# Forgetting attention: VectorE and ScalarE in the order of the program, slabs by halves of 512 tokens, and another split of the PSUM banks

## The chip, the cores and the metric

The kernel runs on one core of a Trainium2 chip. The metric is the device time of one execution in microseconds (us). The profile tells, for each engine of the core, when each instruction ran: PE is TensorE's matmuls and PEld its weight loads, DVE is VectorE, ACT is ScalarE, POOL is GpSimd, and SP issues most of the transfers. Lines such as L180 are lines of the kernel before the change.

## The reference

A trunk of two layers over 1024 tokens of width 1024. Each layer projects its input once into a main branch, memory queries and two gates, runs the main branch and a four-head attention into 256 memory tokens, multiplies both with the SiLU of their gates, projects back and ends in a LayerNorm of `alpha * x + y`. In layer 0 the main branch is a causal pooling over windows of 2, 4, 8 and 16 tokens. In layer 1 it is forgetting attention with 16 heads of 64 channels. Cut to what matters here:

```python
def shared_kv(x, w_kv_shared, b_forget):
    h = x @ w_kv_shared
    k, v = ...                      # 16 heads of 64
    cum = cumsum(log_sigmoid(f_logit + b_forget))
    return k, v, cum

def forgetting_attention(u, k, v, cum):
    logits = einsum('bqhd,bkhd->bhqk', q, k) * 64 ** -0.5
    logits = logits + (cum[t] - cum[s])          # causal: s <= t only
    p = softmax(logits)
    return einsum('bhqk,bkhd->bqhd', p, v)

def mixer_sublayer(x, mem, w_in, w_mem_kv, w_out, main_fn):
    h = x @ w_in                    # [main | mem q | main gate | mem gate]
    y_main, y_mem = main_fn(u_main), memory_attention(q_mem, mem, w_mem_kv)
    y = concatenate([y_main * silu(g_main), y_mem * silu(g_mem)])
    return y @ w_out
```

## The kernel before

**Precision and slabs.** Matmul operands are held as a high and a low part (`hi_lo`: ScalarE casts, VectorE subtracts), and a product is three matmuls: high by high, high by low, low by high. Projections are done in slabs (`slab`): 128 output channels by 1024 tokens, 48 matmuls of 512 columns. A slab's weights come in two pieces of 512 input channels, each a transfer into a `raw` buffer (four of them) and a pair of `w` buffers (six, so three pieces at a time). Outside the attention the pieces are split by ScalarE and VectorE, within it by GpSimd (`gp_hi_lo`, L144 to L146). A slab takes two PSUM accumulators at its start, one for each half of the tokens, and goes through the first piece for both halves, then through the second piece for both.

**PSUM.** There are eight banks: three for slabs (tag `pj`), two for logits (`L`), two for exponentials and transposes (`T`), one for values (`O`).

**Stages.** Layer 0 runs its first pooling group, the memory attention, the other three groups and the output projection with the norm. A pooling group (`pool_group`) is two slabs with a chain of shifted additions on VectorE, two gate slabs, and a mixing of four accumulators of six matmuls each (L518 to L526). Layer 1 runs the memory attention, then a start that makes K and Q of the first pairs of heads, then the attention (`fox`), then `OutProj.rest`. The memory attention and everything from the start of layer 1's heads on has TensorE in the order of the program (`manual_schedule`). VectorE, ScalarE, GpSimd and SP are put in order by the planner of the language, from its own estimates.

**The attention.** `fox` goes through 16 heads, and for each through eight query tiles of 128, from tile 7 down to tile 0. One tile is one step. Heads come in pairs that share slabs of K, Q and V. A step issues `probs`: the mask on the diagonal block of R, the row of forget terms (GpSimd, L716); the logits in one part (up to 512 keys) or two (L722, L723); a VectorE instruction that adds R and takes the running minimum (L724), which reads the logits out of their bank; and after the last part the exponentials on ScalarE into `T` banks, with row sums (L732). `inverse` makes 1/sum of the tile before (VectorE, L740 to L745), and `behind` splits that tile's exponentials into a high half (ScalarE, L753) and a low half (VectorE, L754). `turn` transposes the halves by DMA, and five steps later (`LAG`) `values` multiplies them with V. The values are evicted by ScalarE (L783) and VectorE (L784). Between these, `fill.pump` gives TensorE slab matmuls of the next pair (`pair_units`: a K, a Q and a V slab) and of gates: about 9 to 12 a step. Their evictions are K and Q (`k_evac`, L655 and L656; `q_evac`, L666 and L667), V (a copy, then `scaled_halves`: a maximum, five one-column operations, a high and a low half) and gates (`gate`, L193 and L194). In the last pair the weights of the output projection are split too, with ScalarE and VectorE kept in program order for these alone (`pinned`).

Of the kernel before, what the change touches and what calls it, by code (L numbers as in the profile page):

```python
# [13 lines left out]
I32 = mybir.dt.int32  # L14
# [57 lines left out]
def trunk_kernel(ctx, tc, x, xT, memT, win, wk, wv0, wv, wmk, wmv, wout, poolw, pscale, lng, lnb, bforget, out):  # L72
# [65 lines left out]
    def hi_lo(hi, lo, src, pinned=False):  # L138

        pin = tc.keep_in_program_order if pinned else lambda ins: ins  # L140
        pin(nc.scalar.copy(hi, src))  # L141
        pin(nc.vector.tensor_tensor(lo, src, hi.bitcast(F32), ALU.subtract))  # L142
# [27 lines left out]
    def slab(pieces_dram, XH, XL, evac, banks=("pj", 3)):  # L170

        accs = [ps([P, NH], *banks) for _ in range(2)]
        for pc in range(2):
            ready = isinstance(pieces_dram, list)
            h, l = pieces_dram[pc] if ready else split_w(pieces_dram[pc], [P, 4, P])
            for n in range(2):
                for k in range(4):
                    kt = pc * 4 + k
                    for i, (a, b) in enumerate(((h, XH), (h, XL), (l, XH))):
                        nc.tensor.matmul(  # L180
                            accs[n], a[:, k, :], b[:, kt, n * NH : (n + 1) * NH],
                            start=kt == 0 and i == 0, stop=kt == KT - 1 and i == 2,
                        )
                        if kt == KT - 1 and i == 2:
                            evac(slice(n * NH, (n + 1) * NH), accs[n])
                        since[0] += NH
                        yield NH
# [3 lines left out]
    def gate(acc, dst):  # L191

        nc.scalar.activation(dst, acc, AF.Tanh, scale=0.5)  # L193
        nc.vector.scalar_tensor_tensor(dst, dst, 1.0, acc, ALU.add, ALU.mult)  # L194

    def mem_kv(l):
# [9 lines left out]
        def project(w_dram):  # L206

            acc = ps([P, NH], "pj", 3)[:, :NMEM]
# [16 lines left out]
        def vals(h):  # L225
            scaled_halves(
                project(wmv[l, h]), [two[:, h, 2 * e : 2 * e + 2, :].rearrange("p m t -> p (m t)") for e in range(2)],
                undo[:, h : h + 1],
            )
            if h == MH - 1:  # L230
                nc.sync.dma_start_transpose(v.rearrange("p h b d -> p (h b) d"), two.rearrange("p h b t -> p (h b t)"))
# [3 lines left out]
    def scaled_halves(u, halves, un, by_tile=lambda t: t):  # L235

        m, e, sc = (tiny(1) for _ in range(3))
        nc.vector.tensor_reduce(m, u, AX.X, ALU.max, apply_absolute_value=True)  # L240
        nc.vector.tensor_scalar(m, m, 2.0 ** -100, None, ALU.max)
        nc.vector.tensor_scalar(e.bitcast(I32), m.bitcast(I32), 0x7F800000, None, ALU.bitwise_and)
        nc.vector.reciprocal(sc, e)
        nc.vector.tensor_scalar(sc, sc, 2.0 ** 14, None, ALU.mult)
        nc.vector.tensor_scalar(un, e, 2.0 ** -15 / PSCALE, None, ALU.mult)
        (hi, lo), u = halves, by_tile(u)
        nc.scalar.activation(hi, u, AF.Copy, scale=sc)
        nc.vector.scalar_tensor_tensor(lo, u, sc, hi, ALU.mult, ALU.subtract)
# [14 lines left out]
    def mem_attention(l, XH, XL, kv, qtile, ytile, yd):  # L263
# [18 lines left out]
        def probs(i):  # L282
# [3 lines left out]
            for hp in range(2):  # L286
                lg = ps([P, 2, NMEM], "L", 2)
# [49 lines left out]
    class OutProj:  # L337
# [23 lines left out]
        def split(self, upto, pinned=False):  # L361

            while self.n < upto:
# [6 lines left out]
                hi_lo(h[j], lo[j], self.raws.pop(0), pinned)  # L370
# [19 lines left out]
        def early(self, y, yh, yl):  # L390
# [4 lines left out]
            for two in (slice(0, 2), slice(2, 4)):  # L395
                hi_lo(yh[:, two, :], yl[:, two, :], y[:, two, :], True)
                yield
# [3 lines left out]
        def rest(self, resid, XH, XL, dst):  # L401
# [11 lines left out]
            for sp, c in order + [(sp, c) for sp in range(2, ST // 2) for c in (2, 0, 1)]:  # L413
                if c == 2:
                    accs[sp] = self.open((("T", 2), ("T", 2), ("pj", 3), ("O", 1))) if 0 in accs and sp == 1 else self.open()
# [63 lines left out]
    with tc.tile_pool(name="in0", bufs=1) as in0:  # L479
# [4 lines left out]
        def pool_group(g):  # L484
            w = WINDOWS[g]
            pms = []
            for f in (2 * g, 2 * g + 1):
# [3 lines left out]
                    ("L", 2) if f == 1 else ("pj", 3),  # L491
# [23 lines left out]
            for d in range(2):  # L515
                f = 2 * g + d
                for n in range(2):
                    acc = ps([P, NH], "pj", 3)  # L518
# [24 lines left out]
    with tc.tile_pool(name="in1", bufs=1) as in1:  # L543
# [16 lines left out]
        def values_of(u):  # L560
# [4 lines left out]
            scaled_halves(  # L565
# [3 lines left out]
            for b in range(2):  # L569
                nc.sync.dma_start_transpose(v[:, b, :, :], two[64 * b : 64 * b + 64].rearrange("p s e t -> p (s e t)"))  # L570
# [17 lines left out]
        def v_first():  # L588
# [7 lines left out]
            for s in range(ST):  # L596
                acc = ps([P, NH], "pj", 3)
# [50 lines left out]
        def qk_units(p):  # L648
# [4 lines left out]
            def k_evac(cols, acc):  # L653
                for t, w, (own, other) in zip(ks, ws, halves):
                    nc.scalar.copy(t[own, cols], acc[own, :])  # L655
                    nc.vector.tensor_tensor(t[other, cols], acc[own, :], t[own, cols].bitcast(F32), ALU.subtract)  # L656
                    if cols.stop == S:
                        for to, of in ((own, other), (other, own)):
                            nc.sync.dma_start(w[to, :].bitcast(F32), t[of, :].bitcast(F32))
# [4 lines left out]
            def q_evac(cols, acc):  # L664
                for t, (own, other) in zip(qs, halves):
                    nc.scalar.activation(t[own, cols], acc[own, :], AF.Copy, scale=-0.125)  # L666
                    nc.vector.scalar_tensor_tensor(  # L667
                        t[other, cols], acc[own, :], -0.125, t[own, cols].bitcast(F32), ALU.mult, ALU.subtract,
                    )
# [34 lines left out]
        def probs(hd, i, R, sums, inverse, behind):  # L704
# [16 lines left out]
            for n, (lo, up) in enumerate(parts):  # L721
                lg = ps([P, NH], "L", 2)[:, : up - lo]  # L722
# [3 lines left out]
                if n == 0:  # L726
                    inverse()
            behind()
# [40 lines left out]
        def values(hd, c, o):  # L769
# [14 lines left out]
            nc.vector.scalar_tensor_tensor(oc, acc[own, :], un[own], oc, ALU.mult, ALU.add)  # L784
# [12 lines left out]
        def late_gate(pr):  # L797
# [3 lines left out]
            for c in range(4):  # L801
                cols = slice(c * 2 * P, (c + 1) * 2 * P)
                nc.gpsimd.tensor_tensor(o[:, cols], o[:, cols], g[:, cols], ALU.mult)  # L803
            nc.sync.dma_start(y1d[pr // 4, :, pr % 4, :], o)

        def fox(following, out_proj):
# [8 lines left out]
            for hd in range(HEADS + 1):  # L815
# [15 lines left out]
                for i in range(ST if hd < HEADS else LAG):  # L831
# [7 lines left out]
                    def inverse():  # L839
                        if fresh[0]:  # L840
                            old, k, es, of = fresh[0]
                            fresh[0] = old, k, es, inverse_of(old, k, len(es), of)

# [19 lines left out]
                    else:  # L863
                        inverse()
                        behind()
                    if pr == 7:
                        out_proj.split((0, 0, 0, 1, 2, 3, 4, 5, 5, 5, 5, 6, 6, 6, 7, 8)[step], True)
# [6 lines left out]
                    if older and older[1] % 4 == 0:  # L874
                        values(older[0], older[1] // 4, older[2])
                        if older[0] % 2:
                            pair_out(older[0] // 2, older[1] // 4, older[2], gs.get(older[0] // 2))
                    fill.pump(part * (1 - FRAC[0]))
                    past = past[1:] + [new]
                if b or hd == HEADS:  # L880
                    fill.pump(float("inf"))

        wtags = [("B", 10), ("V", 4), ("MK", 4)] + [("B", 10)] * 3 + [("w", 0), ("MK", 4), ("R", 2), ("V", 4), ("PG", 0), ("B", 10)]
        out_proj = OutProj(1, w_slots(wtags, in1), y1d)
        with tc.manual_schedule(engines={PE}):
# [3 lines left out]
            fox(following, out_proj)  # L889
# [63 lines left out]
```

## Time and profile before

| What | us |
|---|---|
| median of 3 runs | 1256.07 (1255.24 to 1257.23) |
| the profiled execution, its own time | 1256.91 |
| its span, first to last instruction | 1255.2 |
| matmuls busy in the span | 1238.4 |
| first logits of the attention to its last | 673.0 to 1108.3 |

A row of grouped instructions reads: line, engine, operation, what it writes <- what it reads, shapes, count | busy time in us, mean ns of one | idle time of the engine just before these instructions, and who ended it. A row of a timeline reads: start in us, length in us, engine, line, operation, and in square brackets the idle time before it and who ended it. A row of stretches gives, after the stretch and its length, the busy time of PE, PEld, DVE, ACT and POOL with counts, then the granted clock of TensorE, the DMA share and GB/s. A row of waits gives who waited for whom: us in total, how often, the longest.

### The profile page before, as it was taken

What the parts mean: (1) busy time and instruction counts of PE and PEld (TensorE: products, weight loads), DVE (VectorE), ACT (ScalarE), POOL (GpSimd) and SP (SyncE); (2) the same over time, 40 slices, a digit from 0 to 9 for tenths busy, and PEclk for the clock granted to TensorE, in tenths of its full rate; (3) what the DMA queues carried; (4) which work ended last, traced back from release to release, by engine and by line L of the source; (5) the groups of instructions that cost most, each with busy time, mean ns of one, the idle gap of its engine ahead of it and who ended that gap; (6) DMA issues with size and microseconds to landing.
All of it is one profiled execution on the core that took longest, in us unless ns stands there. A gap on an engine that the chain in (4) does not pass through costs nothing. (4 is left out here: it accounts for less than half of the span.)

```text
span 1255.2 us, 19617 instructions
## 1 busy us (share of the span) xinstructions
PE 1238.4 (99%) x7018; PEld 1039.0 (83%) x7018; DVE 797.2 (64%) x1869; ACT 570.4 (45%) x1241; POOL 170.7 (14%) x276
## 2 busy tenths in 40 slices
PE   9999999999999999999999999999999999999997
PEld 7888888888888888888898788887888788888885
DVE  6444766375554456457636778777777788775644
ACT  5233643142321123356324777766766677662110
POOL 0000000000000000000003334333334223430000
PEclk9999999999999999999999999999999999999999
DMA  6333444242362333244516788777867989894530
GB/s 227 109 101 91 120 110 143 85 126 87 115 225 91 104 109 126 85 109 102 175 42 164 155 172 186 181 164 168 176 168 169 177 177 226 207 249 151 178 107 34
DMA packets 267411, 178.65 MB, mean 142 GB/s; under 512 B 212273, under 2 KB 225713, under 8 KB 267313
## 3 DMA queue, kind: packets, MB, share of 16 engines
q1 hardware_dynamic: 267312, 177.40, 53.9%
q8 instruction: 55, 0.90, 0.3%
q14 instruction: 44, 0.35, 0.1%
HBM read 94.97 MB, written 22.61 MB: 94 GB/s over the span
## 5 line engine op out<-in xcount | busy, mean ns | idle before, releaser
L180 PE MATMUL pj<-A,w 128*128 128x512 f32 x2928 | 711.7, 394 | 0.3 <-ACT A L141 0.3
L180 PEld LDWEIGHTS pj<-A,w 128*128 128x128 f32 x2928 | 541.7, 189 | 106.5 <-ACT A L141 1.8
L142 DVE TENSOR_TENSOR w<-raw,w 128x512 fp32r<-128x512 f32 x106 | 73.4, 695 | 106.4 <-ACT w L141 105.6
L732 ACT ACTIVATE T<-MK,s 128x512 f32<-128x512 f32 x192 | 111.1, 578 | 60.6 <-DVE s L724 42.1
L141 ACT CAST w<-raw 128x512 fp32r<-128x512 f32 x106 | 65.6, 621 | 150.3 <-PE pj L180 104.3
L754 DVE SCALAR_TENSOR_TENSOR P<-T,s,P 128x512 f16<-128x512 f32 x192 | 111.9, 613 | 32.4 <-ACT P L753 30.5
L753 ACT ACTIVATE P<-T,s 128x512 f16<-128x512 f32 x192 | 103.6, 576 | 41.3 <-ACT T L732 22.8
L168 PE MATMUL L<-B,B 128*128 128x512 f32 (+3 forms) x384 | 92.4, 345 | 5.0 <-DVE s L724 4.8
L168 PEld LDWEIGHTS L<-B,B 128*128 128x128 f32 x384 | 69.5, 188 | 23.2 <-DVE s L724 11.3
L629 POOL MEMSET G<- 128x128 f32 x1 | 0.2, 205 | 610.4 <-DVE V L334 610.4
L724 DVE CUSTOM_DVE_ANT_0 MK<-L,R 128x512 f32<-128x512 f32 (+3 forms) x128 | 72.8, 569 | 13.5 <-PE L L168 8.3
L142 DVE TENSOR_TENSOR T<-T,T 128x1024 fp32r<-128x1024 f32 x23 | 28.6, 1246 | 68.0 <-PE L L384 51.0
L168 PEld LDWEIGHTS <-V 128*128 128x128 f16 x1152 | 64.4, 98 | 8.8 <-issue 8.1
L146 POOL TENSOR_TENSOR w<-raw,w 128x512 fp32r<-128x512 f32 x54 | 69.6, 1289 | 4.9 <-PE pj L180 1.8
L168 PE MATMUL O<-T,V 128*128 128x128 f16 x1152 | 69.9, 219 | 0.2 <-DMA T<-P 0.2
L141 ACT CAST T<-T 128x1024 fp32r<-128x1024 f32 x23 | 24.2, 1052 | 98.9 <-DMA T<-y0d 50.4
L716 POOL TENSOR_SCALAR_AFFINE_SELECT R<-R 128x128 f32<-128x128 f32 x128 | 42.0, 334 | 170.1 <-DVE s L724 129.4
L145 POOL TENSOR_SCALAR w<-raw 128x512 fp32r<-128x512 f32 x54 | 34.4, 637 | 132.7 <-PE pj L180 132.5
L213 PE MATMUL pj<-T,w 128*128 128x256 f32 x384 | 48.7, 284 | 0.9 <-DVE w L142 0.8
L213 PEld LDWEIGHTS pj<-T,w 128*128 128x128 f32 x384 | 47.5, 191 | 2.0 <-DVE w L142 1.3
L384 PE MATMUL pj<-B,T 128*128 128x512 f32 x186 | 46.1, 391 | 0.0
L384 PE MATMUL L<-B,T 128*128 128x512 f32 x174 | 43.0, 391 | 0.0
(220 smaller groups left out, 1584.5 us busy)
## 6 DMA issues: line engine op xcount, KB each, us to landing
raw<-in_win_dram SPq DMA_DIRECT2D x96, 256.0 KB, 2.8
raw<-in_wout_dram SPq DMA_DIRECT2D x40, 256.0 KB, 2.8
B<-B SPq DMA_DIRECT2D x32, 256.0 KB, 3.4
R<-cumd SPq DMA_DIRECT2D x16, 512.0 KB, 4.4
y0d<-Y SPq DMA_DIRECT2D x12, 512.0 KB, 3.1
T<-y0d SPq DMA_DIRECT2D x12, 512.0 KB, 3.9
T<-y1d SPq DMA_DIRECT2D x11, 512.0 KB, 4.0
raw<-in_wmk_dram SPq DMA_DIRECT2D x16, 256.0 KB, 2.6
```

The lines of the kernel that those rows point to most:

```text
L141: pin(nc.scalar.copy(hi, src))
L142: pin(nc.vector.tensor_tensor(lo, src, hi.bitcast(F32), ALU.subtract))
L146: nc.gpsimd.tensor_tensor(lo, src, hi.bitcast(F32), ALU.subtract)
L168: nc.tensor.matmul(acc, a, b, start=i == 0, stop=i == len(terms) - 1)
L180: nc.tensor.matmul(accs[n], a[:, k, :], b[:, kt, n * NH : (n + 1) * NH], start=kt == 0 and i == 0, stop=kt == KT - 1 and i == 2,)
L213: nc.tensor.matmul(acc, w[:, k, :], m[pc][:, k, :], start=pc == 0 and k == 0 and i == 0, stop=pc == 1 and k == 3 and i == 2,)
L384: nc.tensor.matmul(accs[a][nh], y[:, k, a * P : (a + 1) * P], w, start=kt == 8 and i == 0, stop=kt == 7 and i == 2,)
L716: nc.gpsimd.affine_select(R[:, qs], R[:, qs], [[-1, P]], ALU.is_ge, -NEG, base=0, channel_multiplier=1).ins
L724: nc.vector.tensor_tensor_reduce(p[:, lo:up], lg, R[:, lo:up], 1.0, top, ALU.add, ALU.min, m[:, n : n + 1])
L732: nc.scalar.activation(e, p[:, lo:up], AF.Exp, bias=top, scale=-1.0, accum_out=sums[:, n, hd % 2, i : i + 1],)
L753: nc.scalar.activation(pair[:, lo:up], e, AF.Copy, scale=r)
L754: nc.vector.scalar_tensor_tensor(pair[:, L + lo : L + up], e, r, pair[:, lo:up], ALU.mult, ALU.subtract)
```

## The change

Four things change together.

- **Order.** ScalarE and VectorE are put in program order throughout `fox`. So that this order can be laid out by steps, VectorE's half of an eviction is not issued with ScalarE's half but deferred (`defer`) to a list, `later`, which is emptied (`flush`) in the next step, after the read of the first logits part and the inverse. The scale, high half, low half and transposes of a value slab go on a second list, `slow`, from which the steps of tiles 4 and 3 take. Outside `fox` nothing is deferred.
- **Slabs by 512 tokens.** A slab whose weights come by transfer does the first 512 tokens over both pieces, then the second 512. The very first two slabs, whose pieces are loaded ahead, keep the old order.
- **Banks.** `pj` goes from three to two, `L` from two to three.
- **The output projection** takes its accumulators from `L` and `pj` in turn.

```diff
+    later, slow = [], []
+
+    def defer(what):
+
+        if low[0]:
+            later.append(what)
+        else:
+            what()
+
+    def flush():
+        while later:
+            later.pop(0)()
+
+    def hi_lo(hi, lo, src):
+
+        nc.scalar.copy(hi, src)
+        defer(lambda: nc.vector.tensor_tensor(lo, src, hi.bitcast(F32), ALU.subtract))
...
-    def slab(pieces_dram, XH, XL, evac, banks=("pj", 3)):
+    def slab(pieces_dram, XH, XL, evac, banks=("pj", 2)):
+
+        arrived = isinstance(pieces_dram, list)
+        ws = list(pieces_dram) if arrived else [split_w(pieces_dram[0], [P, 4, P])]
+        accs = {}
+        for n, pc in ((0, 0), (1, 0), (0, 1), (1, 1)) if arrived else ((0, 0), (0, 1), (1, 0), (1, 1)):
+            if len(ws) <= pc:
+                ws.append(split_w(pieces_dram[pc], [P, 4, P]))
+            if n not in accs:
+                accs[n] = ps([P, NH], *banks)
...
         nc.scalar.activation(dst, acc, AF.Tanh, scale=0.5)
-        nc.vector.scalar_tensor_tensor(dst, dst, 1.0, acc, ALU.add, ALU.mult)
+        defer(lambda: nc.vector.scalar_tensor_tensor(dst, dst, 1.0, acc, ALU.add, ALU.mult))
...
-        def open(self, banks=(("pj", 3),) * 2 + (("L", 2),) * 2):
+        def open(self, banks=(("L", 3), ("pj", 2)) * 2):
...
+            goes.append(turned)
+            if low[0]:
+                slow.extend(goes)
+            else:
+                for go in goes:
+                    go()
...
             def k_evac(cols, acc):
+                def lows(acc=acc):
+                    for t, w, (own, other) in zip(ks, ws, halves):
+                        nc.vector.tensor_tensor(t[other, cols], acc[own, :], t[own, cols].bitcast(F32), ALU.subtract)
...
+                for t, (own, other) in zip(ks, halves):
                     nc.scalar.copy(t[own, cols], acc[own, :])
+                defer(lows)
...
-                lg = ps([P, NH], "L", 2)[:, : up - lo]
+                lg = ps([P, NH], "L", 3)[:, : up - lo]
                 mm3(lg, ((q[:, qs], kx[:, lo:up]), (q[:, qs], ky[:, lo:up])))
                 nc.vector.tensor_tensor_reduce(p[:, lo:up], lg, R[:, lo:up], 1.0, top, ALU.add, ALU.min, m[:, n : n + 1])
                 top = m[:, n : n + 1]
                 if n == 0:
                     inverse()
+                    flush()
             behind()
...
             nc.scalar.activation(oc, acc[other, :], AF.Copy, scale=un[own])
-            nc.vector.scalar_tensor_tensor(oc, acc[own, :], un[own], oc, ALU.mult, ALU.add)
+            defer(lambda: nc.vector.scalar_tensor_tensor(oc, acc[own, :], un[own], oc, ALU.mult, ALU.add))
...
                         if fresh[0]:
                             old, k, es, of = fresh[0]
                             fresh[0] = old, k, es, inverse_of(old, k, len(es), of)
+                        if slow and tile_of < 5:
+                            later.append(slow.pop(0))
...
+                    if len(slow) == 3 or len(slow) == 1:
+                        slow.pop(0)()
                     fill.pump(part * FRAC[0])
...
                 if b or hd == HEADS:
                     fill.pump(float("inf"))
+                    flush()
...
-            fox(following, out_proj)
+            with tc.manual_schedule(engines={mybir.EngineType.Activation, mybir.EngineType.DVE}):
+                fox(following, out_proj)
```

`q_evac` is changed as `k_evac` is, and GpSimd's product with a late gate (`late_gate`) and the pair's output (`pair_out`) are deferred in the same way.

More of the change, by code (lines that the diff above doesn't have):

```diff
@@ L664, in q_evac, with lows @@
             def q_evac(cols, acc):
+                def lows(acc=acc):
+                    for t, (own, other) in zip(qs, halves):
+                        nc.vector.scalar_tensor_tensor(
+                            t[other, cols], acc[own, :], -0.125, t[own, cols].bitcast(F32), ALU.mult, ALU.subtract,
+                        )
                 for t, (own, other) in zip(qs, halves):
                     nc.scalar.activation(t[own, cols], acc[own, :], AF.Copy, scale=-0.125)
-                    nc.vector.scalar_tensor_tensor(
-                        t[other, cols], acc[own, :], -0.125, t[own, cols].bitcast(F32), ALU.mult, ALU.subtract,
-                    )
+                defer(lows)
             yield from slab(win[1, p], XH, XL, q_evac)
```

109 lines of the change are left out of this document (54 added, 55 removed).

## The prediction

> **What bounds the kernel now.** I read the page's span and engine rows, then busy time by stretches, then what TensorE waited for.
>
> ```profile
> span 1255.2 us, 19617 instructions
> PE 1238.4 (99%) x7018; PEld 1039.0 (83%) x7018; DVE 797.2 (64%) x1869; ACT 570.4 (45%) x1241; POOL 170.7 (14%) x276
> ...
> core 0: us, PE busy (x) PEld busy (x) DVE busy (x) ACT busy (x) POOL busy (x), PEclk, DMA share, GB/s
> 675.00:1112.00 437.00, 431.73 (x2760) 360.71 (x2760) 344.84 (x983) 305.92 (x706) 154.98 (x255) 1.00 0.82 181
> 1150.00:1175.00 25.00, 25.00 (x112) 20.71 (x111) 15.86 (x28) 3.79 (x5) 0.00 (x0) 1.00 0.44 146
> ...
> PEld L L168 <- DVE s L724: 11.3, 15, 1.5
> ...
> PE L L168 <- DVE s L724: 4.8, 8, 1.1
> ```
>
> TensorE is the bound: 16.8 us of the span are idle. A dense stretch passes 112 matmuls of 512 columns in 25 us, 0.223 us each, without a gap: nothing is to be had there. The attention stage (675 to 1112 us) holds 5.3 us of idle TensorE, 4.8 of it in eight waits of logits matmuls (L168) for VectorE's reading of an earlier logits bank (L724). A matmul row lasts 0.39 us but passes in 0.223, so a wait costs some 0.16 us more than it prints: 4.8 + 8 x 0.16 = 6.1 us. (Fifteen weight loads ahead of logits waited too, 11.3 us; most of that lies under a matmul still running.) The worst one, in order of time:
>
> ```profile
> 862.21 0.21 DVE L742 TENSOR_SCALAR s<-sums 128x1 f32<-128x1 f32 x1 [1.59 <-ACT T L732]
> 862.46 0.16 DVE L745 RECIPROCAL s<-s 128x1 f32<-128x1 f32 x1
> 863.42 0.75 DVE L754 SCALAR_TENSOR_TENSOR P<-T,s,P 128x512 f16<-128x512 f32 x1 [0.80 <-ACT P L753]
> 864.14 0.74 DVE L784 SCALAR_TENSOR_TENSOR G<-O,unscale,G 64x512 f32<-64x512 f32 x1
> 864.80 0.67 DVE L724 CUSTOM_DVE_ANT_0 MK<-L,R 128x512 f32<-128x512 f32 x1
> 865.54 0.73 PE L168 MATMUL L<-B,B 128*128 128x512 f32 x2 [1.09 <-DVE s L724]
> ...
> 867.00:871.20 4.20, 4.20 (x14) 3.32 (x14) 3.74 (x10) 3.63 (x10) 0.34 (x2) 0.59 1.08 254
> ...
> 980.22 0.73 PE L168 MATMUL L<-B,B 128*128 128x512 f32 x2 [1.09 <-DVE s L724]
> ```
>
> VectorE stood idle for 1.59 and 0.80 us, behind a sum and a half that were not ready, while logits lay unread: the planner had put inverse, low half and values eviction ahead of the read. It is an order that stalls, not a full engine: VectorE is busy 345 of 437 us here, ScalarE 306. After that stall the clock was granted at 0.59 for 4.2 us, which cost 4.2 x 0.41 = 1.7 us; an equal stall at 980 us has no such drop on the page.
>
> **The change part by part.** In these rows an engine's next instruction starts before the printed end (863.42 to 864.14 is 0.72 for a row of 0.75; 864.14 to 864.80 is 0.66 for 0.74), so I cost by what passes: printed time less 0.03 to 0.08.
>
> ```profile
> L754 DVE SCALAR_TENSOR_TENSOR P<-T,s,P 128x512 f16<-128x512 f32 x80 | 59.1, 748 | 22.4 <-ACT P L753 21.3
> L724 DVE CUSTOM_DVE_ANT_0 MK<-L,R 128x512 f32<-128x512 f32 x64 | 44.0, 687 | 7.8 <-PE L L168 6.2 <-issue 0.6
> L754 DVE SCALAR_TENSOR_TENSOR P<-T,s,P 128x384 f16<-128x384 f32 x48 | 29.4, 612 | 5.0 <-ACT P L753 4.4
> L754 DVE SCALAR_TENSOR_TENSOR P<-T,s,P 128x256 f16<-128x256 f32 x48 | 22.9, 477 | 3.8 <-ACT P L753 3.8
> L656 DVE TENSOR_TENSOR B<-pj,B 64x512 fp32r<-64x512 f32 x25 | 17.2, 689 | 1.5 <-ACT B L655 0.7
> L248 DVE SCALAR_TENSOR_TENSOR MK<-MK,s,MK 128x1024 f16<-128x1024 f32 x6 | 7.7, 1282 | 1.3 <-ACT MK L247 1.3
> L240 DVE TENSOR_REDUCE s<-MK 128x1 f32<-128x1024 f32 x6 | 7.3, 1220 | 4.3 <-ACT MK L679 4.3
> ...
> L732 ACT ACTIVATE T<-MK,s 128x512 f32<-128x512 f32 x80 | 55.1, 689 | 40.3 <-DVE s L724 28.0 <-DVE P L754 12.1
> L753 ACT ACTIVATE P<-T,s 128x512 f16<-128x512 f32 x80 | 53.9, 685 | 30.4 <-ACT T L732 18.1 <-issue 8.5 <-DVE s L745 1.4
> L732 ACT ACTIVATION_READ_ACCUMULATOR T<-MK,s 128x1 f32 x192 | 36.2, 189 | 0.2
> L732 ACT ACTIVATE T<-MK,s 128x384 f32<-128x384 f32 x48 | 27.6, 575 | 4.4 <-DVE s L724 2.3 <-DVE P L754 1.7
> L732 ACT ACTIVATE T<-MK,s 128x256 f32<-128x256 f32 x48 | 22.4, 467 | 9.9 <-DVE s L724 6.7 <-DVE P L754 3.3
> L666 ACT ACTIVATE B<-pj 64x512 fp32r<-64x512 f32 x28 | 16.5, 588 | 7.4 <-DVE B L667 6.5 <-PE pj L180 0.7
> ```
>
> (1) Program order. No instruction is added; VectorE's order per step becomes: read of the first logits part, inverse of the tile before, the deferred low parts, read of the second part, low halves of the tile before. The read comes first, so the stall above cannot recur in that form: -6.1 us at most, and with it the clock drop, -1.7. But now the engines wait for each other in a fixed ring: inverse 0.50 (0.21 + 0.16 and starting), first high half 0.69, first low half 0.72, which frees the T bank, then the exponentials: 0.75 and 0.575 + 0.19 for tile 6. That is 3.4 us; the values' low part (0.66 to 0.74) ahead of the second read makes it 3.9. Tile 5 so takes 3.3; tile 4 3.2, or 4.8 where the scale of the value slab (1.22 and five one-column operations like the 0.16 above) is flushed ahead of its second read; tile 3, by VectorE's work, inverse 0.45 + K low parts 2 x 0.66 + value low half 1.25 + low halves 1.03 + next read 0.53 = 4.6; tiles 2, 1, 0 and 7 take 2.4, 2.6, 2.1, 2.7: 26.4 us for the first head of a pair. The second has Q's low parts, 1.3 us, at tiles 7 and 3: 4.0 + 3.9 + 3.3 + 3.2 + 3.3 + 2.4 + 2.0 + 2.1 = 24.2. Against that stands TensorE's own pace, read from the first logits of four heads whose pairs have three slabs to fill with:
>
> ```profile
> 946.20 0.39 PE L168 MATMUL L<-B,B 128*128 128x512 f32 x1
> ...
> 971.36 0.61 PE L168 MATMUL L<-B,B 128*128 128x512 f32 x2
> ...
> 1024.35 0.39 PE L168 MATMUL L<-B,B 128*128 128x512 f32 x1
> ...
> 1049.10 0.62 PE L168 MATMUL L<-B,B 128*128 128x512 f32 x2
> ```
>
> Head 10 (946.20 to 971.36) and head 13 (1024.35 to 1049.10) ran undisturbed: 25.2 + 24.7 = 49.9 us, against 50.6 for the ring. Four pairs (1, 3, 5, 6) are like this; pairs 2, 4 and 7 have a fourth slab or more, 10.9 us (48 x 0.223 and some) of TensorE time, beside at most 1.4 us of gate low parts on VectorE, and pair 0 has no value slab. The ring falls behind in tiles 4 and 3 by (4.8 + 4.6) less two steps of 3.1, some 3.2 us, and catches up in the light ones.
>
> (2) Three logits banks. A logits part then waits for the read three parts earlier, not two: with two parts in a heavy step, one and a half steps of about 3.5 us, 5 us, may be lost before TensorE waits. The 3.2 us fit; adding the 0.7 per pair that is not recovered, and following the second head's tiles 7 to 5 part by part, I find one wait of 0.5 us per such pair: +2.0 us in all (from 0, if the lag fits everywhere, to 8, if each such pair loses 2).
>
> (3) Two banks for slabs, halves one after the other. Each 512-token half now ends 24 matmuls (5.4 us) after the other, and a bank is wanted again only then, against an eviction of 0.6 + 0.7 us: no wait. Both weight pieces of a slab are wanted within 12 matmuls; a piece's buffer is free 24 matmuls before (it was 48), and its preparation is short:
>
> ```profile
> L142 DVE TENSOR_TENSOR w<-raw,w 128x512 fp32r<-128x512 f32 x20 | 13.8, 690 | 26.2 <-ACT w L141 26.2
> L141 ACT CAST w<-raw 128x512 fp32r<-128x512 f32 x20 | 12.5, 623 | 45.5 <-PE pj L180 40.9 <-issue 4.3 <-ACT T L141 0.3
> ...
> L496 DVE TENSOR_TENSOR G<-G 128x1020 f32<-128x1020 f32 x4 | 4.9, 1220 | 0.1
> ...
> L146 POOL TENSOR_TENSOR w<-raw,w 128x512 fp32r<-128x512 f32 x52 | 67.0, 1289 | 4.8 <-PE pj L180 1.8
> L716 POOL TENSOR_SCALAR_AFFINE_SELECT R<-R 128x128 f32<-128x128 f32 x128 | 42.0, 334 | 170.1 <-DVE s L724 129.4 <-DVE s L745 31.2 <-DVE s L744 7.5
> L145 POOL TENSOR_SCALAR w<-raw 128x512 fp32r<-128x512 f32 x51 | 31.7, 621 | 76.9 <-PE pj L180 76.7
> ...
> 332.44 1.75 PE L168 MATMUL pj<-T,MK 128*128 128x512 f32 x7
> ...
> 333.27 0.69 DVE L194 SCALAR_TENSOR_TENSOR Y<-Y,pj 128x512 f32<-128x512 f32 x1 [0.83 <-ACT Y L193]
> ```
>
> A piece takes 0.62 + 0.69 = 1.3 us on ScalarE and VectorE, in the attention stage 0.62 + 1.29 = 1.9 on GpSimd, out of 5.4: hidden. What could take that cover away is VectorE's run of pooling work, at most six instructions of 1.22 us, 7.3 us, if it stood ahead of the low part; a group would then lose some 2 us. But it starts when a slab ends, and the next slab's second piece became free 12 matmuls, 2.7 us, before that end and needs 1.3; I take 0. GpSimd and the SP queue carry the same transfers, only a slab's second one 12 matmuls earlier. Where a wait does come is the four pool mixings: their second group of six matmuls starts 6 x 0.223 = 1.34 us after 332.44, at 333.78, in the bank that the gate eviction leaves only at 333.96. About 0.25 us each, +1.0 us (0 to 2).
>
> (4) On GpSimd the mask (0.33 us) of a later tile now stands close behind a weight split whose buffer TensorE frees 1 to 10 matmuls before that tile's logits: the mask may come 1.7 us late. It is wanted by the second read, 0.7 to 3 us later in the ring, so I take 0. The last stage only exchanges banks; its tail keeps its order: 0.
>
> Sum against the profiled run, 1256.9 us (span 1255.2): -6.1 - 1.7 + 2.0 + 1.0 = -4.8, so 1252.1; that run lies 0.8 above the median of 1256.07, so on the median's scale 1251.3: I say 1251.
>
> "TensorE: Matmul & The Clock Gate" of the Trainium skill (Part 1) states half clock after a whole idle window of about 3.4 us. The waits before the drop here printed 1.09 us and less, so the trace shows a drop after less idle time than that; by the rule the drop is not the stall's, and the sum would be 1253.
>
> **The rivals.** (a) The old waits are traded for as many new ones: the ring is late in all four pairs and each loses 1.7 us (6.8 in all): 1256, no change. For it: 50.6 against 49.9. (b) The ring becomes the bound: its dependencies cost 0.25 us a step more than I count, by high halves that come late behind slab evictions on ScalarE (L666, 0.59 each, two in a row, ahead of the halves in its order). From 51.6 us per pair, 1.7 over TensorE's, it eats the whole gain; at 16 x 0.25 more it is 54.6, 4.7 per pair, 18.8 in all, of which the 5 us of slack hide little: 1256.1 - 6.8 + 18.8 - 5 = 1263, slower. Against it: VectorE's 79% load. (c) Slab banks bound TensorE: each of the 62 slabs of the program waits 0.2 us at its handover, as at the mixings: +12.4 less 6.8, 1262. Against it: 5.4 us of cover. "A second HAM failure mode: psum-queue depth-cycling" on the same page of the Trainium skill describes such small idle times making the clock swing; no row here shows it for slabs. (d) All waits of the stage go, none comes, and 2 of the further us in which weight loads waited for a read (11.3 against 4.8) come back too: 1256.1 - 7.8 - 2 = 1246.
>
> **How the numbers follow.** Forecast 0.52, (a) 0.17, (b) 0.17, (c) 0.05, (d) 0.09. Within 0.2% (2.5 us, about what a measurement of this kernel can tell) is (a); faster is the forecast, but for the end of its span, and (d), 0.61; slower (b) and (c), 0.22. The likeliest case spans 1248 to 1255 by its terms' bounds (waits 0 and 0, or 5 and 2); to leave out no more than 2 in 10 the range is 1246 to 1263.
>
> **What would show it.** Right: TensorE's waits for the logits reads in the attention stage under 2.5 us, VectorE's read of the first part starting each step, no granted clock under 0.9 there, short gaps of 0.2 to 0.3 us at the second mixing group of each pool group. Wrong: waits of 0.5 us or more at tiles 5 to 3 of most heads, or slab matmuls waiting for evictions or weight splits.

## The result, and the profile after

The changed kernel takes 1265.09 us (median of 6 runs, 1264.40 to 1266.78) against 1255.9 us before (6 runs, 1254.63 to 1257.29). The ratio is 1.0073, with a 95% interval of 1.0063 to 1.0082: slower by 0.7%. The prediction was 1251 us and faster; both its direction and its range missed.

First the span and engine rows of the page after, then busy time by the same four stretches of both kernels: the first 25 us, up to the first logits of the attention, to its last logits, and the rest. The kernel after:

```profile
span 1265.1 us, 19628 instructions
PE 1238.6 (98%) x7018; PEld 1038.0 (82%) x7018; DVE 794.4 (63%) x1869; ACT 567.1 (45%) x1241; POOL 167.4 (13%) x276
...
0.00:25.00 25.00, 22.17 (x75) 15.66 (x76) 13.61 (x33) 12.46 (x15) 0.70 (x6) 1.00 0.72 255
25.00:678.20 653.20, 650.55 (x3538) 549.76 (x3537) 362.19 (x725) 227.13 (x484) 4.41 (x6) 1.00 0.38 111
678.20:1118.20 440.00, 427.85 (x2748) 358.32 (x2747) 339.96 (x972) 299.55 (x697) 154.69 (x256) 1.00 0.81 179
1118.20:1265.10 146.90, 138.03 (x663) 114.28 (x661) 78.64 (x140) 27.98 (x46) 7.63 (x8) 0.98 0.44 142
```

The kernel before:

```profile
0.00:25.00 25.00, 23.46 (x84) 16.83 (x85) 14.19 (x35) 13.97 (x19) 0.70 (x6) 1.00 0.72 263
25.00:673.00 648.00, 646.88 (x3528) 548.41 (x3527) 361.23 (x724) 225.46 (x482) 5.19 (x6) 1.00 0.38 112
673.00:1108.30 435.30, 430.03 (x2748) 359.47 (x2747) 342.04 (x975) 303.29 (x698) 156.86 (x256) 1.00 0.82 181
1108.30:1255.20 146.90, 138.06 (x663) 114.31 (x662) 79.80 (x137) 27.70 (x46) 7.96 (x8) 0.98 0.42 138
```

TensorE does the same work (7018 matmuls, 1238 us) and idles 10 us more. The last stretch is 146.90 us in both. The attention, the same 2748 matmuls, takes 440.0 us in place of 435.3: +4.7, though the clock drop of the kernel before is gone (its 1.7 us came back). The other 5.2 us lie ahead of it: about 2 us in the first 25 us, where 9 matmuls fewer had passed, 1.8 us in the pool mixings, and some 1.3 us that was not traced further. The 2 us at the start belong to this one execution: the six runs below that have the same start (runs 4 to 9) passed 86 to 90 matmuls in those 25 us, and the profiled execution lies 1.7 us above the median of its kernel.

What TensorE waited for in the kernel after (engine, line and tile waited for: us in total, times, longest):

```profile
PE pj L196 <- DVE B L687: 6.9, 5, 1.7
PE pj L196 <- DVE B L702: 2.9, 4, 1.2
PE L L180 <- DVE s L763: 2.3, 3, 1.4
PE pj L196 <- ACT A L153: 1.6, 1, 1.6
PE pj L180 <- DVE Y L210: 1.4, 3, 0.5
```

The one wait for L153 stands at 7.5 us, in the first stretch. The waits for the logits reads (L763, L724 before) fell from 4.8 to 2.3 us. In their place slab matmuls (L196) wait for K's and Q's low parts (L687, L702), which are the last readers of a slab bank: 9.8 us in nine waits, which the kernel before does not have at all. Three of the four mixings wait for the gate's low part (L210), each time behind a weight split (L154) on VectorE; the first:

```profile
54.28 0.69 DVE L154 TENSOR_TENSOR w<-raw,w 128x512 fp32r<-128x512 f32 x1 [1.99 <-ACT w L153]
54.89 0.68 DVE L210 SCALAR_TENSOR_TENSOR Y<-Y,pj 128x512 f32<-128x512 f32 x1
...
55.62 0.73 PE L180 MATMUL pj<-T,MK 128*128 128x512 f32 x2 [0.45 <-DVE Y L210]
```

One such wait in order of time; it is the second half of a slab of K, at tiles 4 to 1 of head 4:

```profile
795.47 1.22 DVE L258 TENSOR_REDUCE s<-MK 128x1 f32<-128x1024 f32 x1
...
797.18 0.39 PE L196 MATMUL pj<-A,w 128*128 128x512 f32 x1
...
797.96 1.14 DVE L794 SCALAR_TENSOR_TENSOR P<-T,s,P 128x512 f16<-128x512 f32 x2
798.74 0.59 ACT L772 ACTIVATE T<-MK,s 128x384 f32<-128x384 f32 x1 [3.65 <-DVE P L794]
799.85 1.13 ACT L268 ACTIVATE MK<-MK,s 128x1024 f16<-128x1024 f32 x1
802.86 0.69 ACT L772 ACTIVATE T<-MK,s 128x512 f32<-128x512 f32 x1 [1.06 <-DVE P L794]
803.58 1.17 ACT L693 CAST B<-pj 64x512 fp32r<-64x512 f32 x2
804.79 1.41 DVE L687 TENSOR_TENSOR B<-pj,B 64x512 fp32r<-64x512 f32 x2 [0.72 <-ACT B L693]
806.34 1.83 PE L196 MATMUL pj<-A,w 128*128 128x512 f32 x7 [1.49 <-DVE B L687]
```

The half is complete at 797.57 (797.18 + 0.39). Its copies take 1.17 us and its low parts 1.41, but ScalarE starts the copies at 803.58: in program order they stand behind the exponentials (L772), which wait for the low halves of the tile before (L794) to leave the two T banks, and those had waited in VectorE's order behind the value slab's scale (L258 and what follows). The low parts end at 806.20, 8.6 us after the half. TensorE wanted the bank at 804.85 (806.34 less the wait of 1.49), 7.3 us after the half, and stood.

### The profile page after: what moved, and what is told of

The parts are those of the page before. It is cut to its first block, busy times and chain, and to the rows that moved or that the text cites. A ratio compares the mean times of both kernels' runs of the same rounds, so it can differ in the third digit from the quotient of the medians.

```text
span 1265.1 us, 19628 instructions
## 1 busy us (share of the span) xinstructions
PE 1238.6 (98%) x7018; PEld 1038.0 (82%) x7018; DVE 794.4 (63%) x1869; ACT 567.1 (45%) x1241; POOL 167.4 (13%) x276
## 5 line engine op out<-in xcount | busy, mean ns | idle before, releaser
L196 PE MATMUL pj<-A,w 128*128 128x512 f32 x2928 | 712.9, 393 | 11.4 <-DVE B L687 6.9
L196 PEld LDWEIGHTS pj<-A,w 128*128 128x128 f32 x2928 | 539.9, 188 | 120.6 <-issue 9.6
L772 ACT ACTIVATE T<-MK,s 128x512 f32<-128x512 f32 x192 | 110.8, 577 | 74.1 <-DVE P L794 52.5
L154 DVE TENSOR_TENSOR w<-raw,w 128x512 fp32r<-128x512 f32 x106 | 73.0, 690 | 94.5 <-ACT w L153 93.8
L794 DVE SCALAR_TENSOR_TENSOR P<-T,s,P 128x512 f16<-128x512 f32 x192 | 112.4, 613 | 23.9 <-ACT P L793 23.0
L153 ACT CAST w<-raw 128x512 fp32r<-128x512 f32 x106 | 65.6, 620 | 122.4 <-PE pj L196 78.2
L763 DVE CUSTOM_DVE_ANT_0 MK<-L,R 128x512 f32<-128x512 f32 (+3 forms) x128 | 72.6, 567 | 26.7 <-PE L L180 22.6
L154 DVE TENSOR_TENSOR T<-T,T 128x1024 fp32r<-128x1024 f32 x23 | 28.5, 1239 | 64.3 <-PE pj L406 51.5
L153 ACT CAST T<-T 128x1024 fp32r<-128x1024 f32 x23 | 24.2, 1051 | 97.2 <-DMA T<-y0d 53.2
```

Of the source, the lines that this page charges most:

```text
L154: defer(lambda: nc.vector.tensor_tensor(lo, src, hi.bitcast(F32), ALU.subtract))
L196: nc.tensor.matmul(accs[n], a[:, k, :], b[:, kt, n * NH : (n + 1) * NH], start=kt == 0 and i == 0, stop=kt == KT - 1 and i == 2,)
L763: nc.vector.tensor_tensor_reduce(p[:, lo:up], lg, R[:, lo:up], 1.0, top, ALU.add, ALU.min, m[:, n : n + 1])
L772: nc.scalar.activation(e, p[:, lo:up], AF.Exp, bias=top, scale=-1.0, accum_out=sums[:, n, hd % 2, i : i + 1],)
L794: nc.vector.scalar_tensor_tensor(pair[:, L + lo : L + up], e, r, pair[:, lo:up], ALU.mult, ALU.subtract)
```

## The experiments

A number used below is the time from the end of a half's last matmul (its start and 0.39 us) to the end of its last low part, over the 12 halves of K that the attention makes. In the kernel before its mean is 4.6 us, after the change 6.9, at most 9.0.

**1. The banks put back.** Three slab banks and two logits banks, all else as changed.

```diff
-banks=("pj", 2) ... ps([P, NH], "L", 3)
+banks=("pj", 3) ... ps([P, NH], "L", 2)
```

> The changed kernel with the banks of before (three for slabs, two for logits, the last stage's four likewise); orders and halves stay. Theory A, two slab banks are too few for evictions that program order makes late: the slab matmuls' waits for K's and Q's low parts (6.9 + 2.9 us in 9 waits, 11.2 us with 0.16 each) and the mixings' (1.4 us in 3) go, and two logits banks cost some back: waits for the logits reads of 3 to 8 us in place of 2.3. 1253 to 1258 us. Rival B, the fixed order of VectorE and ScalarE itself holds TensorE up whatever the banks: the waits move to the logits, 10 us or more there, 1262 us or more.

Measured: 1262.42 us, ratio 1.0051 (1.0034 to 1.0067). No slab wait is left in the attention and the mixings no longer wait, but the attention still takes 439.7 us:

```profile
PE L L180 <- DVE s L763: 6.7, 8, 2.3
PE L L180 <- DVE s L784: 1.9, 1, 1.9
```

In the second row an inverse (L784) was the last that they waited for. So two slab banks alone, theory A, are not the cause. With a third bank K's low parts still end 6.7 us behind their half in the mean; the banks decide whether a slab or a logits part is the one to wait. Rival B came out right in time, its 10 us of waits being 8.6 us.

**2 and 3. The rest of the change without the order.** First halves and banks, then halves alone, both put into the kernel before with nothing deferred and both engines in the planner's order.

```diff
-accs = [ps([P, NH], *banks) for _ in range(2)]; for pc in range(2): for n in range(2):
+for n, pc in ((0, 0), (0, 1), (1, 0), (1, 1)):      # as in the change
-("pj", 3), ("L", 2)
+("pj", 2), ("L", 3)                                 # run 2 alone
```

> The kernel before with the slabs by 512 tokens and two banks for slabs, three for logits; VectorE and ScalarE in the planner's order, nothing deferred. Theory A (late evictions by program order are what two slab banks don't cover): no slab wait over 0.3 us in the attention stage, since evictions go when they are ready; mixing waits as in the changed kernel (1.4 us printed); logits waits 1 to 4 us in place of 4.8: 1253 to 1257 us. Rival C, two slab banks are too few in any order: 5 us or more of waits of slab matmuls, 1261 us or more.

> The kernel before with slabs by 512 tokens alone (three slab banks, two logits banks, planner's order). Theories A and B both: no more than 1 us either way of 1256 us. Rival D, the order by halves costs by itself, by weight pieces that are wanted 12 matmuls earlier: waits of slab matmuls for weight splits, 1258 us or more.

Measured: 1251.51 us with both, ratio 0.9962 (0.9947 to 0.9977), and 1251.67 us with halves alone, 0.9966 (0.9953 to 0.9979). Both are faster than before. With both, no slab matmul of the attention waits and the attention is done in 427.1 us; the mixings' three waits are there. That rules out C and D. That halves alone would gain 4 us was in no theory; 1256 was expected. The same half of K in the run with both:

```profile
790.17 1.07 PE L184 MATMUL pj<-A,w 128*128 128x512 f32 x4
...
793.26 0.57 ACT L659 CAST B<-pj 64x512 fp32r<-64x512 f32 x1
793.86 0.68 DVE L660 TENSOR_TENSOR B<-pj,B 64x512 fp32r<-64x512 f32 x1
...
795.56 0.58 ACT L659 CAST B<-pj 64x512 fp32r<-64x512 f32 x1
...
796.17 0.69 ACT L736 ACTIVATE T<-MK,s 128x512 f32<-128x512 f32 x1
796.40 0.69 DVE L660 TENSOR_TENSOR B<-pj,B 64x512 fp32r<-64x512 f32 x1
```

The half ends at 791.24, and the planner slips each copy in ahead of the next exponential; the bank is free 5.9 us later, not 8.6. The mean for K is 4.2 us.

**4 and 5. One engine at a time.** The changed kernel with program order for VectorE alone, then for ScalarE alone.

```diff
-with tc.manual_schedule(engines={Activation, DVE}):
+with tc.manual_schedule(engines={DVE}):          # run 4; {Activation} in run 5
```

> The changed kernel with ScalarE's order left to the planner, VectorE's in program order. If it is ScalarE's order that makes the evictions late (K's high parts stood behind the exponentials, 803.58 us for a half that ended before 799), waits for K's and Q's low parts fall from 9.8 to under 4 us: 1256 to 1261 us. If it is VectorE's (low parts deferred to the next step's flush, behind the value slab's scale), they stay at 8 us or more: 1263 to 1267 us.

> The changed kernel with ScalarE in program order and VectorE left to the planner. With VectorE's order alone the time was 1257.9 us, with no order (halves and banks only) 1251.5, with both 1265.1. If the two costs add, ScalarE's alone is worth 7 us: 1257 to 1260 us. If they hurt only together, by waiting on each other in a ring, 1251 to 1254 us.

Measured: VectorE's order alone 1257.92 us, ratio 1.0016 (1.0006 to 1.0025); ScalarE's alone 1267.93 us, 1.0097 (1.0083 to 1.0111). With ScalarE free, the waits for K's and Q's low parts are 3.1 us in place of 9.8; with ScalarE fixed and VectorE free they are 7.4. Run 4, then run 5:

```profile
PE pj L196 <- DVE B L687: 2.5, 4, 1.3
...
PE pj L196 <- DVE B L702: 0.6, 1, 0.6
```

```profile
PE pj L196 <- DVE B L687: 3.9, 4, 2.2
PE pj L196 <- DVE B L702: 3.5, 4, 1.5
```

ScalarE's order is what makes the copies late: K's start 0.7 us behind their half in run 4, 4.1 in run 5 and 4.3 in the changed kernel (means). The low parts are late without it too, since they are deferred: 6.2 us in run 4 against 6.9, but none later than 7.7, against 9.0.

Both runs defer as the changed kernel does, so what they are to be held against is not run 2 but run 8 below (1260.7 us, the deferral with neither order fixed). Against it ScalarE's order costs 7.3 us alone and 7.2 beside VectorE's, and VectorE's gains 2.7 alone and 2.8 beside ScalarE's: on the medians the two add up, though the executions of run 8 spread over 6 us. Where they cost is not the same: some 4 us of run 5's loss lie in the last stage, whose first products wait 2.1 us for ScalarE and go on at half clock, which no other run shows.

**6. The flush moved behind the low halves.**

```diff
                 if n == 0:
                     inverse()
-                    flush()
             behind()
+            flush()
```

> The changed kernel with the flush (deferred low parts, value slab's scale) issued behind the low halves of the tile before, not between the two logits reads. Theory E, the flush stands in the ring: at 793.5 to 797.5 us K's low parts and the scale held the second read, and so the low halves, for 4 us, and ScalarE's exponentials with K's next high parts behind them waited 3.65 us. Then most waits of slab matmuls for low parts and of logits for reads go: 1255 to 1260 us. Rival F, the bank is held by low parts that come late, and later still now: waits for K's and Q's low parts above 10 us, 1266 us or more. Rival G, the order costs what it costs wherever the flush stands: 1263 to 1266 us.

Measured: 1281.27 us, ratio 1.0196 (1.0179 to 1.0212). This is what rival F expected:

```profile
PE pj L196 <- DVE B L687: 13.8, 9, 3.1
```

K's low parts now end 8.6 us behind their half. In this order, what frees a slab bank cannot be put later.

**7. The low parts not deferred.**

```diff
-                defer(lows)             # for K and for Q; the gates' low part likewise
+                lows()
```

> The changed kernel with the low parts of K, Q and the gates issued right behind ScalarE's parts instead of at the next flush; both engines in program order. If the deferral is what holds the slab banks (rival F of the run with the flush moved), the waits for K's and Q's low parts fall from 9.8 to under 4 us: 1256 to 1261 us. If ScalarE's copies are late in their own order, VectorE now waits for them with the reads and halves behind: no gain or a loss, 1264 to 1272 us.

Measured: 1293.62 us, ratio 1.0305 (1.0291 to 1.0319), worse than any expectation. The low parts end later too, 7.8 us behind their half in the mean, and now the logits reads, queued behind low parts that wait for ScalarE's copies, are late as well:

```profile
PE pj L196 <- DVE B L687: 13.2, 8, 2.7
PE L L180 <- DVE s L763: 10.3, 8, 2.0
```

Of the 28.5 us beyond the changed kernel some 10 go to a lower granted clock, 0.54 to 0.66 in five stretches of 24.5 us together. Neither later nor earlier helps while ScalarE's order is fixed: the copies themselves come late, behind exponentials that wait.

**8. Deferred, but in the planner's order.**

```diff
-with tc.manual_schedule(engines={Activation, DVE}):
-    fox(following, out_proj)
+fox(following, out_proj)
```

> The changed kernel with neither engine held to program order; low parts and the value slab's scale are still written out a step later. If the fixed orders are the cost, it comes to the run with halves and banks alone, 1251 to 1253 us, and K's low parts end some 4 us behind their half (mean 4.2 us there, 6.9 in the changed kernel). If the deferral costs by itself, because the planner too places what is written later behind what is written before it, 1256 us or more, with K's low parts at 6 us or more.

Measured: 1260.65 us (1258.75 to 1264.79), ratio 1.0041 (1.0024 to 1.0059). The first expectation is wrong. The second has the time right, and nearly K's low parts, but what TensorE waits for is mostly not a slab bank:

```profile
PE O L180 <- DMA T<-P: 3.5, 1, 3.5
PE L L180 <- DVE s L763: 3.4, 3, 1.7
...
PE pj L196 <- DVE B L687: 0.9, 2, 0.5
```

K's low parts end 5.7 us behind their half; the slab waits are 0.9 us, but once turned probabilities come 3.5 us late to the values' matmuls, and logits reads are late by 3.4 us. The attention takes 435.6 us, 8.5 more than in run 2. Of these, 5.1 lie in head 13, where that one wait is and the granted clock is 0.66 from 1025 to 1030 us, and 2.2 in head 15, in the last pair: there run 2 has the splits of the output projection's weights in program order (`pinned`), and this run has not. So not all of the 9 us is shown to be the deferral's, and why the planner's order came out that way was not followed further.

**9. The value slab's scale moved from tile 4 to tile 2.**

```diff
-                        if slow and tile_of < 5:
+                        if slow and tile_of < 3:
```

> The changed kernel with the value slab's scale put into the flush at tile 2 instead of tile 4. Theory E', the scale (2 us of VectorE between two reads, just as the first half of K waits to be evicted) is the last straw for K's bank: the waits of 1.66, 1.65 and 1.84 us for K's low parts at tile 2 of heads 4, 8 and 12 go, at most a third of them comes back elsewhere (values late by their transposes): 1260 to 1263 us. If program order is a step late with or without the scale: the waits stay over 1 us, 1264 to 1267 us.

Measured: 1270.06 us, ratio 1.0109 (1.0086 to 1.0132). The waits of 1.49 and 1.48 us at tile 1 of heads 4 and 8 (1.66 and 1.65 with what a wait costs beyond its print) are gone, so the scale was their last straw, but in head 12 slab matmuls still wait for K's low parts, up to 2.0 us, and the values' matmuls wait for the transposed value slab:

```profile
PE O L180 <- DMA V<-MK: 7.4, 4, 5.0
PE pj L196 <- DVE B L687: 3.0, 2, 2.0
```

More than was won is lost on the other side of the step, part of it by a granted clock of 0.53 from 1030 to 1041 us; the expectation missed the size of it.

**10. A third T bank in place of the third logits bank.** Both engines in program order, everything deferred, as in the change.

```diff
-ps([P, NH], "T", 2) ... ps([P, NH], "L", 3)
+ps([P, NH], "T", 3) ... ps([P, NH], "L", 2)
```

> The changed kernel with three banks for the exponentials and two for logits. If the exponentials' wait for the low halves (52.5 us of ScalarE's idle time) is the link that makes the slab evictions behind them late, K's low parts end a low half sooner (mean 6.9 to about 6.2 us), the waits for K's and Q's low parts fall from 9.8 us to under 6; two logits banks cost 3 to 6 us of waits there: 1260 to 1266 us. If not, the slab waits stay at 9 us or more and the logits waits come on top: 1267 us or more.

Measured: 1255.99 us, ratio 1.0004 (0.9994 to 1.0014): 9.1 of the 9.2 us that the change lost are back, by one bank moved from the logits to the exponentials, and more than was expected. The group of the exponentials on the page of the changed kernel (busy, mean ns | idle time before them, and who ended it):

```profile
L772 ACT ACTIVATE T<-MK,s 128x512 f32<-128x512 f32 x192 | 110.8, 577 | 74.1 <-DVE P L794 52.5
```

and on that of this run, with its slab waits and the same half of K:

```profile
L772 ACT ACTIVATE T<-MK,s 128x512 f32<-128x512 f32 x192 | 111.4, 580 | 34.9 <-DVE s L763 33.6
...
PE L L180 <- DVE s L763: 2.4, 2, 2.2
...
PE pj L196 <- DVE B L687: 1.2, 2, 0.9
...
791.76 0.84 PE L196 MATMUL pj<-A,w 128*128 128x512 f32 x3
...
795.83 0.69 ACT L772 ACTIVATE T<-MK,s 128x512 f32<-128x512 f32 x1
796.54 1.18 ACT L693 CAST B<-pj 64x512 fp32r<-64x512 f32 x2
...
798.11 1.41 DVE L687 TENSOR_TENSOR B<-pj,B 64x512 fp32r<-64x512 f32 x2
```

The exponentials no longer wait for the low halves, so the copies behind them start 3.9 us after their half (792.60 to 796.54) in place of 6.0 (797.57 to 803.58). K's mean falls from 6.9 to 5.4 us, and the waits for its low parts and Q's from 9.8 to 1.2 us. Against run 1 only one bank differs, moved from slabs to T, and that is worth 6.4 us: three slab banks do not cure what a third T bank does.

**11 and 12. The mixings in the logits banks, and a third T bank in the planner's order.** Run 2 with the pool mixings in the three logits banks; then that with three T and two logits banks.

```diff
-                    acc = ps([P, NH], "pj", 2)
+                    acc = ps([P, NH], "L", 3)      # the mixings of pool_group
```

> The kernel before with halves and two and three banks (1251.5 us), and the pool mixings' four groups in the three logits banks in place of the two slab banks. The mixings' three waits (0.61 us of lost TensorE time each) go and nothing else changes: 1249 to 1250.5 us, faster than before by 0.4 to 0.5%. If the gate evictions' bank was wanted next by a slab instead, the waits come there: 1251.5 us.

> The fastest so far (halves, two slab banks, mixings in the logits' banks, planner's order: 1249.3 us) with three banks for the exponentials and two for logits. In the fixed order this move of a bank took 9 us off. If a third bank there matters only where the order is fixed, because the planner puts the evictions ahead of exponentials that wait, nothing is left to gain: 1249 to 1252 us, the logits' waits (1.1 us) up by 0 to 2. If the exponentials' bank holds up either order, 1248 us or less.

Measured: 1249.27 us (1248.04 to 1252.57), ratio 0.9954 (0.9940 to 0.9967), and 1252.60 us (1249.21 to 1256.35), 0.9980 (0.9968 to 0.9993). The mixings' waits are gone, and the first is the fastest of all; its attention takes 426.8 us. The third T bank gains nothing where the planner orders the engines and nothing is deferred, and is rather a loss (1252 us was the end of what was expected). It was not tried with the deferral in the planner's order, so whether it cures the fixed order alone is not shown.

## Why the prediction was wrong

**The step that failed** is (3), two banks for slabs: "against an eviction of 0.6 + 0.7 us: no wait". The duration of one instruction is right (0.58 and 0.70), though a half of K or Q has two of each, 1.17 + 1.41. The cover was even longer than the 5.4 us: in the chain shown, 7.3. What was left out is the place of the eviction in the queues. The text had priced the ring of the two engines in step (1), with the two T banks in it and the scale of the value slab at tile 4, and had a lag of 3.2 us in tiles 4 and 3. That lag is there (ScalarE waited 3.65 us). But it was held against the logits banks alone; the slab evictions that step (1) itself had put into the ring were priced in step (3) as if they ran at once. They end 6.9 us behind their half in the mean: ScalarE's order holds the copies behind exponentials that wait for a T bank (runs 4 and 10), and the deferral puts the low parts a step later. Nine waits, 9.8 us printed and 11.2 with 0.16 each, stand where the sum had 0.

**The other terms.**
- The logits waits: -6.1 was "at most" and +2.0 came as ring waits, together -4.1. By the same working, three waits of 2.3 us are left, 2.8 with 0.16 each: -3.3. They sit in heads 0 and 2, not at tiles 7 to 5 of second heads. (The likeliest case took 5 us as the most that they could come to, where step (2) had allowed 8; with 8 it would have reached 1258.) Three logits banks do give the tolerance that step (2) gave them: with two, run 1, the waits are 8.6 us.
- The clock: -1.7 came in this execution, whose attention shows a granted clock of 1.00. But not every execution of the kernel before seems to have the drop: 30 of its runs show a mean granted clock of 0.998 and a median of 1254.9 us, 14 show 0.995 or 0.996 and 1256.9. The text took off the drop, and then the 0.8 us by which that execution lay above the median, which is probably in part the same time. Nor does the order keep the clock up: runs 1, 6, 7, 9 and 10, with both orders fixed, have drops in the attention.
- The mixings: +1.0 was priced as four waits of 0.25. There are three, each printed at 0.45 and costing 0.61 with what a wait costs beyond its print, since on VectorE a weight split of 0.69 us stands ahead of the gate's low part: 1.8.
- The slabs by halves: the text gave them no gain of their own. Run 3, with nothing else changed, is 3.9 us faster than the kernel before.
- Weight pieces, GpSimd's masks and the last stage at nothing: right. No wait for a weight split or mask stands in the attention, and the last stretch has the same 146.90 us.
- The sum as it came: -3.3 - 1.7 + 11.2 + 1.8, and 2.0 for the start of this execution, is 10.0; the spans differ by 9.9. That it fits so closely is partly luck: the attention's three terms make 6.2 where it lost 4.7, and some 1.3 us ahead of it have no term. Between the medians, 9.2 us apart, the start falls away and 8.0 is left; without the drop, which most executions of the kernel before do not seem to have, it is 9.7. The profiled execution before, with its drop, was 1.0 us above its own median.

**The rivals.** (c) named the right resource, the slab banks, and the sign, but as a toll of 0.2 us at each of 62 handovers; it came as nine waits of 1.1 us in light tiles (2 to 0), where nothing was looked for. (b) named the ring and ScalarE's order, yet as late high halves behind the evictions; it was the evictions that came late. In heads without a wait the steps still take the pace of TensorE (25.2 us for three slabs), so the ring is not too long for a step in the mean; it is some of its evictions that come too late. The signs that the text set down as proof against it were the right ones: slab matmuls waiting for evictions.

**What is shown and what is not.** That ScalarE's fixed order makes the copies late through the T banks, and that most of the slab waits come of it, is shown by runs 4 and 10, with runs 1 and 5 beside them. Split by medians, halves and banks are worth -4.1 us (run 2), and the way from there to the changed kernel is +9.1 for the deferral (run 8, with the reservation made there), -2.7 for VectorE's order (run 4) and +7.2 for ScalarE's on top. So the deferral may be the larger part. Its chain was not followed, and with the orders fixed, leaving it out for K, Q and the gates is worse (run 7). Why halves alone make the kernel before 4 us faster is not settled: its two worst stalls, at 865 and 980 us, are gone in run 3, which has another of 2.8 us at 679.

## What to carry to other kernels

Price an eviction by when its instruction comes up in its engine's queue, not by how long it takes: in a fixed order, everything issued behind an instruction that waits for a bank inherits the wait, and the buffer that runs short can be a different one from the buffer that is tight. When a change fixes an order and regroups buffers at the same time, ask of each buffer who frees it and what stands ahead of that reader in the new order. Before spending banks where the waits are printed, look for the link that is waited for one step earlier; here one bank more for the exponentials returned 9 us, and one more for the slabs 2.7, each taken from the logits. And when an order is fixed and work is put off to fit it, measure the putting off alone: here the run with it alone has 9.1 of the 13.6 us between run 2 and the changed kernel.

## What the runs showed of the hardware

The granted clock fell to half for three to four us (0.57 in the mean of 4 us) behind single short waits of TensorE. Four rows of stretches show it (the clock is the third number from the end), of run 1, of run 6 with a second row, of run 10 and of run 12:

```profile
679.00:683.00 4.00, 3.65 (x9) 2.77 (x10) 2.71 (x10) 2.19 (x6) 0.33 (x2) 0.57 0.86 218
```

```profile
748.00:752.00 4.00, 3.52 (x10) 2.93 (x11) 3.07 (x10) 2.40 (x6) 0.66 (x2) 0.57 0.62 148
...
680.00:686.00 6.00, 4.62 (x22) 3.89 (x23) 3.86 (x12) 2.91 (x7) 0.88 (x3) 1.00 0.77 181
```

```profile
681.00:685.00 4.00, 3.80 (x11) 2.91 (x10) 2.67 (x9) 2.90 (x7) 0.58 (x2) 0.57 0.83 188
```

```profile
679.00:683.00 4.00, 3.95 (x12) 2.85 (x11) 2.19 (x9) 3.17 (x8) 0.58 (x2) 0.57 0.92 218
```

The waits that ended ahead of or in the rows at 0.57 were 2.3, 2.4, 2.2 and 1.8 us long. A wait of 2.3 us at 681 us of run 6 has no drop behind it (the row at 1.00), nor has any wait in the attention of the changed kernel, of at most 1.7 us. Before the change, two waits of 1.09 and 0.46 us, ended at 865.5 and 866.7 us, came ahead of the row at 0.59 that the prediction shows. So no one length decides here. A drop costs 4 x 0.43 = 1.7 us more, and run 6 has four of them, from 748, 809, 929 and 1041 us. The Trainium skill, in "TensorE: Matmul & The Clock Gate" (Part 1), asks for an idle window of about 3.4 us; the trace does not agree, since waits of 1.8 to 2.4 us were enough in these runs.
